# Order and sources of the first loads, casts and squares of a hybrid decoder trunk on one core

## Chip, core and metric

The kernel runs on one core of one Trainium2 chip. The metric is the device time of one execution in microseconds (us), the median of several runs; less is better. A profile of one execution, with every instruction's start and length and every DMA, is there as well.

## What is computed

The reference is a trunk of two layers over 528 positions (16 learned meta tokens ahead of 512 inputs) with 1024 features. Layer 0 is a sliding-window attention and a Mamba-2 scan side by side, layer 1 a convolution module; a squared-ReLU MLP follows each. What matters here is how layer 0 begins:

```python
h = jnp.concatenate([meta, x], axis=1)
u = rms_norm(h, norm_g)          # h * rsqrt(mean(h*h) + EPS) * norm_g
proj = u @ w_in                  # 1024 -> 3088 columns
q, k, v, z, xbc, dt_raw = jnp.split(proj, ...)
```

## The kernel before

All activations lie with features on the 128 partitions (8 feature tiles k) and positions along the free axis. Positions are cut into two streams: stream 0 has 272, stream 1 has 256 (STREAM, L28). Every large product is done in float32r with both operands cut into a high part and a low rest: hi·xh + hi·xl + lo·xh, that is 3 matmuls per feature tile (`products`, L518: first the pairs hi·xh and hi·xl for each k, then the lo·xh of the same piece). A weight comes in pieces of 4 feature tiles (256 KB): a DMA into a buffer `wr`, a cast on ScalarE (ACT) into the high part `wh` (`th_cast`, L464), and a subtraction on VectorE (DVE) or GpSimd (POOL) for the low rest `wl` (`th_low`, L480). There are four buffers of each kind at this point; `wh` and `wl` are given back when TensorE (PE) has used the piece for both streams.

The input goes through the same split. `th_enter` (L663) makes, for each k of a stream, xh = h·g on ACT (L671) and xl = h·g − xh on DVE (L672); g is `norm_g`, of which the first 8 columns of `vec` are loaded ahead of everything else (L1883). `th_norm` (L681) squares each k on ACT and adds the squares up on DVE (`sumsq`, L637); `row_norm` (L594) sums over the partitions on PE, takes square root (ACT) and reciprocal (DVE), and spreads the result to a tile `rb`. The row factor is thus not applied to the input but to the products: `ev_in` (L773) multiplies a finished output tile by `rb` when both streams' `rb` are there, and only then the PSUM bank of the product is free. PSUM has 8 banks: 3 called "mm" and 2 called "at", which take the products here, and 3 called "bg" for background work such as `row_norm` and `th_dt`. `pmm` (L346) takes an "mm" bank, or a "bg" bank when `wide[0]` allows it.

`main` (L1637) starts with `warm` (L1628), matmuls of a zeroed tile into a bank that nothing reads. It then computes output tiles 0 and 1 for stream 0 (L1658), the same two for stream 1 (L1665), and each further tile for both streams in turn (L1672). `extra` (L1645) says which input loads go ahead of which weight piece; `th_load` (L443) issues all loads on one queue, SyncE's (SP).

The order of instructions on each engine is not written out by hand. Generators ("threads") yield operations with an estimated length, and `Sched.step` (L178) simulates the engines and emits the operation that could start first; among those that could start at the same time it takes the one whose thread has the lowest priority number. The estimate for a load is 1500 ns of latency, then 5.2 ns per KB one after the other, then 700 ns (L129, L298). These estimates thus decide the order of all later instructions of the program, not only of the loads.

Of the kernel before, what the change touches and what calls it, by code (L numbers as in the profile page):

```python
# [9 lines left out]
F32 = mybir.dt.float32  # L10
F32R = mybir.dt.float32r
BF16 = mybir.dt.bfloat16
AF = mybir.ActivationFunctionType
# [226 lines left out]
def trunk(ctx: ExitStack, tc: tile.TileContext, h0, vecs, cmat, atab, atab0, w_in, w_dt, w_out,  # L240
# [20 lines left out]
    def TT(o, a, b, op, pool=False):  # L261
        n = cols(o)
        ways = [("V", 1.04 * n + 145, lambda: nc.vector.tensor_tensor(o, a, b, op=op), sb(a) and sb(b))]  # L263
        if pool:
            ways.append(("G", 2.17 * n + 170, lambda: nc.gpsimd.tensor_tensor(o, a, b, op=op), True))  # L265
        return Op(ways, [o], [a, b])
# [12 lines left out]
    def VEC(ns, fn, o, *inp, port=False):  # L279
        return Op([("V", ns, fn, port)], o if isinstance(o, list) else [o], list(inp))  # L280
# [7 lines left out]
    def CP(o, a):  # L288
        return Op([("A", 0.836 * cols(o) + 192, lambda: nc.scalar.copy(o, a), False)], [o], [a])  # L289
# [5 lines left out]
        return Op([("G", 1.1 * cols(o) + 170, lambda: nc.gpsimd.tensor_copy(o, a), True)], [o], [a])  # L295

    def DMA(o, a, kb):
        return Op([("S", kb * 5.2, lambda: nc.sync.dma_start(o, a), False)], aps(o) if sb(o) and o.tensor.name in S.mem else [],  # L298
                  [a] if a.tensor.name in S.mem else [])

    def load(o, a, kb):
# [39 lines left out]
    def bank(tag, name):  # L341
        return take(ps, [128, 512], F32, tag, BANKS[tag], name)
# [81 lines left out]
    def th_sum():  # L424
        i = 0
        while True:
            yield lambda: i < len(plan) or over
            if i >= len(plan):
                return
            if plan[i][3] == "sum":  # L430
                op, (a, x), (b, y) = plan[i][1]
                yield lambda: a in raws and b in raws
                t = yield take(wm, [128, 4, 128], F32, "raw", 4, "ws")
                o = TT(t, raws[a][:, x:x + 4], raws[b][:, y:y + 4], op, True)
                o.ways[0] += (bias[0] / 2,)
                yield o
                raws[i] = t
                used_raw(a, b)
            i += 1

    extra = {}

    def th_load():  # L443
        i = 0
        while True:
            yield lambda: i < len(plan) and plan[i][0] in POOLS or over
            if over and i >= len(plan):
                return
            for g in extra.pop(i, ()):
                yield from g  # L450
            pool, src, n, kind = plan[i]
            if kind in (None, "raw"):
                p, nraw, nsplit, w = POOLS[pool]
                raw = yield take(p, [128, w, 128], F32, "raw", nraw, "wr")
                yield DMA(raw[:, :n], src, 64 * n)
                raws[i] = raw
            i += 1

# [5 lines left out]
    def th_cast():  # L464
        i = 0
        while True:
            yield lambda: i < len(plan) or over
            if i >= len(plan):
                return
            if plan[i][3] != "raw":  # L470
                j, src = source(i)
                yield lambda: j in raws
                pool, _, n, _ = plan[i]
                p, nraw, nsplit, w = POOLS[pool]
                hi = yield take(p, [128, w, 128], F32R, "hi", nsplit, "wh")
                yield CP(hi[:, :n], src())
                his[i] = hi
            i += 1

    def th_low():  # L480
        i = 0
        while True:
            yield lambda: i < len(plan) or over
            if i >= len(plan):
                return
            if plan[i][3] != "raw":
                yield lambda: i in his
                pool, _, n, _ = plan[i]
                p, nraw, nsplit, w = POOLS[pool]
                lo = yield take(p, [128, w, 128], F32R, "lo", nsplit, "wl")  # L490
                j, src = source(i)
                hi = his.pop(i)
                o = TT(lo[:, :n], src(), hi[:, :n].bitcast(F32), ALU.subtract, True)
                o.ways[0] += (bias[0],)
                yield o
                used_raw(j)
                ready[i] = (hi, lo)
                split[0] += 1
            i += 1
# [122 lines left out]
    def par(gens, prio, name):  # L622

        left = [0]

        def run(g):
            yield from g
            left[0] -= 1
        for g in gens:
            left[0] += 1  # L630
            spawn(run(g), prio, name)
        yield lambda: left[0] == 0

    def after(*names):
        return lambda: all(n in done for n in names)
# [27 lines left out]
    def th_enter(s):  # L663

        n = STREAM[s][1]

        def one_(k):
            g = V("g_mix", k)
            hk = hin[s][:, k, :n]
            yield after(f"hin{s}{k}")  # L670
            yield ACT(xh[s][:, k, :n], hk, AF.Copy, scale=g)  # L671
            yield STT(xl[s][:, k, :n], hk, g, xh[s][:, k, :n].bitcast(F32), ALU.mult, ALU.subtract)  # L672
            entered[s].add(k)
        yield from par([one_(k) for k in range(8)], 2 * s, "enter")
        yield after(f"sq{s}")
        drop(hin[s])
        sz[s] = yield K(f"kl{s}", F32, f"sz{s}")
# [3 lines left out]
    def th_norm(s):  # L681
        n = STREAM[s][1]
        begun = []

        def one_(k):
            yield after(f"hin{s}{k}")
            yield from sumsq(acc[s], hin[s][:, k, :n], k == 0, begun)
        yield from par([one_(k) for k in range(8)], 1 + 2 * s, "norm")
        done.add(f"sq{s}")
        r = yield from row_norm(s, acc[s], BLOCKS[s], 1e-6, f"in{s}")  # L690
        done.add(f"rb{s}")
        yield VCP(rtok[:, BLOCKS[s][0]:BLOCKS[s][-1] + 1], r)
        done.add(f"rtok{s}")
# [558 lines left out]
    def load_h(s, k, n):  # L1252
        c0, w = STREAM[s]
        yield load(hin[s][:, k:k + n, :w], h0[:, k:k + n, c0:c0 + w], 0.5 * n * w)
        for j in range(k, k + n):
            done.add(f"hin{s}{j}")
# [371 lines left out]
    def warm():  # L1628

        z = at.rearrange("p h k -> p (h k)")[:, 0:512]  # L1630
        yield VEC(300, lambda: nc.vector.memset(z, 0.0), z)
        p = yield bank("at", "warm")
        for _ in range(11):
            yield Op([("P", 430, lambda: nc.tensor.matmul(p, lhsT=z[:, 0:128], rhs=z, start=True, stop=True), False)], [p], [z])
        drop(p)

    def main():  # L1637
# [4 lines left out]
        expect([w_out[n, :, 4:] for n in range(8)], 8)  # L1642
        plan_mlp(0, 0, 2, 4, 2, 4)
        plan_mlp(0, 1, 0, 0, 2, 4)
        extra.update({0: [load_h(0, 0, 1)], 1: [load_h(0, 1, 1), load_h(0, 2, 2)], 2: [load_h(0, 4, 2), load_h(0, 6, 2)],  # L1645
                      4: [load_h(1, 0, 2), load_h(1, 2, 2), load_h(1, 4, 2), load_h(1, 6, 2), load_const()],
                      5: [run_th(th_dtw(), "dtw")], 8: [run_th(tables(), "tables")]})
        for s in range(2):
# [6 lines left out]
        spawn(th_ssd_norm(), 1, "ssd_norm")  # L1655
        X = [(xh[s], xl[s], 0, STREAM[s][1]) for s in range(2)]
        lead = []
        for n in range(2):  # L1658
            p = yield bank("mm", "in")
            pcs = []  # L1660
            for k in (0, 4):
                pcs.append((yield from piece()))
                yield from products(p, pcs[-1], k, range(k, k + 4), 8, X[0], 0, lambda k: k in entered[0])
            lead.append((p, pcs))
        for n in range(2):  # L1665
            p, pcs = lead[n]
            q = yield bank("at", "in")
            for k, pc in zip((0, 4), pcs):
                yield from products(q, pc, k, range(k, k + 4), 8, X[1], 0, lambda k: k in entered[1])
                done_with(*pc[:2])  # L1670
            spawn(ev_in(n, (p, q)), 1, "inev")
        for n in ORDER[2:]:  # L1672
            b, pcs = [], []
            for s in range(2):
                p = yield bank("mm", "in")
                b.append(p)
                for i, k in enumerate((0, 4)):
                    if s == 0:
                        pcs.append((yield from piece()))
                    yield from products(p, pcs[i], k, range(k, k + 4), 8, X[s])  # L1680
                    if s:
                        done_with(*pcs[i][:2])
            spawn(ev_in(n, b), 1, "inev")
# [196 lines left out]
        yield from mlp(1, 3, [(*F[0], *AH[0], None), (*F[1], *AH[1], None)], last=fin_part)  # L1880

    with tc.manual_schedule():
        nc.sync.dma_start(vec[:, 0:8], vecs[:, 0:8])  # L1883
        S.part(vec)[0][0][:, :8] = 2500.0
        for g, p, n in ((main(), 5, "main"), (th_load(), 0, "load"), (th_cast(), 1, "cast"), (th_sum(), 1, "sum"),
                        (th_low(), lambda: 1 if split[0] - used[0] < 3 else 4, "low")):
            spawn(g, p, n)
        while S.threads:
            S.step()
# [84 lines left out]
```

## Time and profile before

| | |
|---|---|
| runs of the kernel before | 1229.56 us median of 3 (1229.52 to 1231.16) |
| profiled execution | 1230.29 us, of which the span from first to last instruction is 1228.5 us |
| PE busy | 1213.2 us (99% of the span) |
| DVE, ACT, POOL busy | 869.2, 714.7, 532.5 us |
| bytes moved by DMA | 185.98 MB, mean 151 GB/s |
| mean granted TensorE clock | 0.997 |

Times within the profile count from the first instruction. In a row of the timeline stand: start, length in us, engine, line, operation, output and inputs by the program's names, shapes, a count, and in square brackets the idle time ahead of it and what ended it. A row with a count covers that many instructions and its length is from the first's start to the last's end. Consecutive instructions of an engine overlap, so that the distance of two starts is shorter than one length. A row of the chain of waits has start, length and what was on the chain.

### The profile page before, as it was taken

How to read it: one execution, taken by the hardware profiler on the slowest of the kernel's cores; microseconds unless marked ns; L12 is line 12 of the kernel's file. 1: busy time of each engine (PE TensorE's matmuls, PEld its weight loads, DVE VectorE, ACT ScalarE, POOL GpSimd, SP SyncE). 2: the span in 40 equal slices, each digit the busy share in tenths (PEclk: the TensorE clock that was granted, in tenths of full speed). 3: DMA queues.
4: the chain of work that ended last, by engine and by line, in shares of the span. 5: the costliest groups of instructions: out<-in, count | busy, mean ns of one | idle time of the engine just before them, and what ended most of it. 6: DMA issues, size and time to landing. Idle time of an engine off the chain costs nothing.

```text
span 1228.5 us, 25576 instructions
## 1 busy us (share of the span) xinstructions
PE 1213.2 (99%) x9891; PEld 1169.4 (95%) x9891; DVE 869.2 (71%) x1921; ACT 714.7 (58%) x1391; POOL 532.5 (43%) x335
## 2 busy tenths in 40 slices
PE   8999999899999999999999999999999999999998
PEld 7999887689999999999999999999999999999998
DVE  6745686776876575748999735499996676666687
ACT  7654246767665654564664677557556665544452
POOL 0212331352542121158888788788887600000123
PEclk9999999999999999999999999999999999999999
DMA  6323112335445765546565565565555656556222
GB/s 192 106 81 89 41 37 77 97 96 163 130 146 182 235 194 165 185 125 194 184 189 175 170 190 176 178 200 175 180 181 174 192 159 194 189 183 190 87 62 94
DMA packets 76793, 185.98 MB, mean 151 GB/s; under 512 B 8560, under 2 KB 16256, under 8 KB 76672
## 3 DMA queue, kind: packets, MB, share of 16 engines
q1 hardware_dynamic: 76672, 184.36, 48.8%
q8 instruction: 77, 1.26, 0.4%
q14 instruction: 44, 0.36, 0.1%
HBM read 182.23 MB, written 2.10 MB: 150 GB/s over the span
## 4 chain that ended last, share of the span: by engine, by line
PE 93%; ACT 3%; DVE 3%; issue 1%; DMA 0%; SPq 0%; DVEq 0%; ACTq 0%
PE in L317 12%; PE pw L317 9%; PE out L317 6%; PE up13AB L317 4%; PE dn13AB L317 3%; PE dn00A L317 2%; PE up01A L317 2%; PE up02A L317 2%; PE dn01A L317 2%; PE up00A L317 2%; PE up03A L317 2%; PE dn02A L317 2%; PE dn02B L317 2%; PE up10A L317 2%; PE up12A L317 2%; PE dn12B L317 2%
## 5 line engine op out<-in xcount | busy, mean ns | idle before, releaser
L265 POOL TENSOR_TENSOR wl<-wr,wh 128x512 fp32r<-128x512 f32 x275 | 486.8, 1788 | 579.4 <-ACT wh L289 501.2
L289 ACT CAST wh<-wr 128x512 fp32r<-128x512 f32 (+1 forms) x472 | 367.6, 797 | 244.4 <-issue 27.5
L263 DVE TENSOR_TENSOR wl<-wr,wh 128x512 fp32r<-128x512 f32 (+1 forms) x197 | 183.8, 943 | 94.7 <-ACT wh L289 92.6
L270 DVE SCALAR_TENSOR_TENSOR conv<-U,vec,conv 128x256 f32<-128x256 f32 x464 | 209.2, 486 | 9.6 <-ACT conv L285 2.7
L317 PE MATMUL in<-xh,wh 128*128 128x272 f32 (+1 forms) x384 | 104.0, 297 | 1.5 <-ACT wh L289 1.5
L317 PE MATMUL in<-xl,wh 128*128 128x272 f32 (+1 forms) x384 | 100.9, 289 | 1.3 <-DVE xl L270 1.3
L317 PE MATMUL pw<-nh,wh 128*128 128x256 f32 (+1 forms) x320 | 80.7, 286 | 0.1
L317 PE MATMUL pw<-nl,wh 128*128 128x256 f32 (+1 forms) x320 | 80.2, 284 | 0.0
L317 PEld LDWEIGHTS in<-xh,wh 128*128 128x128 f32 x384 | 73.4, 191 | 6.8 <-issue 3.4
L317 PEld LDWEIGHTS in<-xl,wh 128*128 128x128 f32 x384 | 73.5, 191 | 2.5 <-DVE xl L270 2.1
L317 PE MATMUL in<-xh,wl 128*128 128x272 f32 (+1 forms) x384 | 66.5, 291 | 0.0
L317 PEld LDWEIGHTS pw<-nh,wh 128*128 128x128 f32 x320 | 60.2, 188 | 0.5 <-ACT sqh L285 0.3
L317 PEld LDWEIGHTS pw<-nl,wh 128*128 128x128 f32 x320 | 60.3, 189 | 0.0
L317 PEld LDWEIGHTS in<-xh,wl 128*128 128x128 f32 x384 | 54.8, 192 | 1.5 <-issue 0.7
L317 PE MATMUL pw<-nh,wl 128*128 128x256 f32 (+1 forms) x320 | 48.1, 284 | 0.0
L317 PEld LDWEIGHTS pw<-nh,wl 128*128 128x128 f32 x320 | 42.7, 188 | 0.0
L285 ACT ACT_TABLE_LOAD x30 | 38.5, 1283 | 5.5 <-DMA hin<-in_h 3.9
L317 PE MATMUL out<-xh,wh 128*128 128x272 f32 (+1 forms) x128 | 33.3, 289 | 0.5 <-ACT h L289 0.5
L317 PE MATMUL out<-xl,wh 128*128 128x272 f32 (+1 forms) x128 | 32.7, 284 | 0.0
L263 DVE TENSOR_TENSOR pw<-pw,rb 128x272 f32<-128x272 f32 (+1 forms) x32 | 14.0, 439 | 26.0 <-PE pw L317 25.7
L317 PE MATMUL up13AB<-nl,wh 128*128 128x256 f32 x128 | 31.1, 281 | 0.0
L317 PE MATMUL up13AB<-nh,wh 128*128 128x256 f32 x128 | 31.1, 281 | 0.0
(604 smaller groups left out, 3667.9 us busy)
## 6 DMA issues: line engine op xcount, KB each, us to landing
wr<-in_w_dn SPq DMA_DIRECT2D x80, 512.0 KB, 3.9
wr<-in_w_up SPq DMA_DIRECT2D x78, 512.0 KB, 3.6
wr<-in_w_up SPq DMA_DIRECT2D x84, 256.0 KB, 4.3
wr<-in_w_dn SPq DMA_DIRECT2D x80, 256.0 KB, 4.0
wr<-in_w_p SPq DMA_DIRECT2D x36, 512.0 KB, 3.7
wr<-in_w_in SPq DMA_DIRECT2D x48, 256.0 KB, 2.9
wr<-in_w_out SPq DMA_DIRECT2D x36, 256.0 KB, 2.7
wr<-in_w_p SPq DMA_DIRECT2D x24, 256.0 KB, 4.7
```

Source lines behind the costliest of these rows:

```text
L263: ways = [("V", 1.04 * n + 145, lambda: nc.vector.tensor_tensor(o, a, b, op=op), sb(a) and sb(b))]
L265: ways.append(("G", 2.17 * n + 170, lambda: nc.gpsimd.tensor_tensor(o, a, b, op=op), True))
L270: lambda: nc.vector.scalar_tensor_tensor(o, a, s, b, op0=op0, op1=op1), sb(a) and sb(b))],
L285: return Op([("A", ns, lambda: nc.scalar.activation(o, a, f, **kw), False)], aps(o, accum), aps(a, scale, bias), table=TABLE.get(f, 0))
L289: return Op([("A", 0.836 * cols(o) + 192, lambda: nc.scalar.copy(o, a), False)], [o], [a])
L317: nc.tensor.matmul(o, lhsT=l, rhs=r, start=st, stop=sp)
```

## The change

- `warm`: after the zero tile is set, ACT takes the square root of one column of it; 8 matmuls of zeros instead of 11.
- The first 8 columns of `vec` (the norm's scales, 4 KB) are loaded by ACT's queue instead of SP's.
- The first weight piece is loaded, cast and subtracted in two halves of two feature tiles; the load of k = 1 of stream 0 goes between the halves.
- `th_norm`: the squares of stream 0 may begin when all 8 tiles of stream 0 and 2 of stream 1 are split, those of stream 1 when all of both are. Before, a square could begin as soon as its tile had landed.
- Priorities: the split of stream 1 goes from 2 to 0.8, the casts from 1 to 0.7.
- The third output tile may take one "bg" bank for its second stream.
- The estimate of a load goes from 5.2 to 3.4 ns per KB, for every load of the program.
- `for n in range(2)` becomes `ORDER[:2]`, which holds the same two tiles.

```diff
     def DMA(o, a, kb):
-        return Op([("S", kb * 5.2, lambda: nc.sync.dma_start(o, a), False)], ...
+        return Op([("S", kb * 3.4, lambda: nc.sync.dma_start(o, a), False)], ...
...
+    def parts_of(i, n):
+
+        return ((0, n),) if i else ((0, n // 2), (n // 2, n))
...
-                yield DMA(raw[:, :n], src, 64 * n)
+                for a, b in parts_of(i, n):
+                    yield DMA(raw[:, a:b], src[:, a:b], 64 * (b - a))
+                    for g in extra.pop((i, b), ()):
+                        yield from g
...
-                yield CP(hi[:, :n], src())
+                for a, b in parts_of(i, n):
+                    yield CP(hi[:, a:b], src()[:, a:b])
...
-                o = TT(lo[:, :n], src(), hi[:, :n].bitcast(F32), ALU.subtract, True)
-                o.ways[0] += (bias[0],)
-                yield o
+                for a, b in parts_of(i, n):
+                    o = TT(lo[:, a:b], src()[:, a:b], hi[:, a:b].bitcast(F32), ALU.subtract, True)
+                    o.ways[0] += (bias[0],)
+                    yield o
...
-        yield from par([one_(k) for k in range(8)], 2 * s, "enter")
+        yield from par([one_(k) for k in range(8)], 0.8 * s, "enter")
...
         def one_(k):
-            yield after(f"hin{s}{k}")
+            yield lambda: len(entered[0]) == 8 and len(entered[1]) >= (8 if s else 2)
             yield from sumsq(acc[s], hin[s][:, k, :n], k == 0, begun)
...
         yield VEC(300, lambda: nc.vector.memset(z, 0.0), z)
+        yield ACT(small([128, 1], "then"), z[:, 0:1], AF.Sqrt)
         p = yield bank("at", "warm")
-        for _ in range(11):
+        for _ in range(8):
...
-        extra.update({0: [load_h(0, 0, 1)], 1: [load_h(0, 1, 1), load_h(0, 2, 2)], ...
+        extra.update({0: [load_h(0, 0, 1)], (0, 2): [load_h(0, 1, 1)], 1: [load_h(0, 2, 2)], ...
...
         for n in ORDER[2:]:
+            wide[0] = 1 if n == ORDER[2] else 0
             b, pcs = [], []
             for s in range(2):
-                p = yield bank("mm", "in")
+                p = yield pmm("in")
...
-        nc.sync.dma_start(vec[:, 0:8], vecs[:, 0:8])
+        nc.scalar.dma_start(vec[:, 0:8], vecs[:, 0:8])
...
-        for g, p, n in (... (th_cast(), 1, "cast"), ...
+        for g, p, n in (... (th_cast(), 0.7, "cast"), ...
```

More of the change, by code (lines that the diff above doesn't have):

```diff
@@ L297, in DMA @@
     def DMA(o, a, kb):
-        return Op([("S", kb * 5.2, lambda: nc.sync.dma_start(o, a), False)], aps(o) if sb(o) and o.tensor.name in S.mem else [],
+        return Op([("S", kb * 3.4, lambda: nc.sync.dma_start(o, a), False)], aps(o) if sb(o) and o.tensor.name in S.mem else [],
                   [a] if a.tensor.name in S.mem else [])
@@ L1644, in main @@
         plan_mlp(0, 1, 0, 0, 2, 4)
-        extra.update({0: [load_h(0, 0, 1)], 1: [load_h(0, 1, 1), load_h(0, 2, 2)], 2: [load_h(0, 4, 2), load_h(0, 6, 2)],
+        extra.update({0: [load_h(0, 0, 1)], (0, 2): [load_h(0, 1, 1)], 1: [load_h(0, 2, 2)], 2: [load_h(0, 4, 2), load_h(0, 6, 2)],
                       4: [load_h(1, 0, 2), load_h(1, 2, 2), load_h(1, 4, 2), load_h(1, 6, 2), load_const()],
@@ L1657, in main @@
         lead = []
-        for n in range(2):
+        for n in ORDER[:2]:
             p = yield bank("mm", "in")
@@ L1664, in main @@
             lead.append((p, pcs))
-        for n in range(2):
-            p, pcs = lead[n]
+        for n, (p, pcs) in zip(ORDER, lead):
             q = yield bank("at", "in")
@@ L1882, in trunk @@
     with tc.manual_schedule():
-        nc.sync.dma_start(vec[:, 0:8], vecs[:, 0:8])
+        nc.scalar.dma_start(vec[:, 0:8], vecs[:, 0:8])
         S.part(vec)[0][0][:, :8] = 2500.0
-        for g, p, n in ((main(), 5, "main"), (th_load(), 0, "load"), (th_cast(), 1, "cast"), (th_sum(), 1, "sum"),
+        for g, p, n in ((main(), 5, "main"), (th_load(), 0, "load"), (th_cast(), 0.7, "cast"), (th_sum(), 1, "sum"),
                         (th_low(), lambda: 1 if split[0] - used[0] < 3 else 4, "low")):
```

## The prediction

> **What bounds the kernel now.** I read the page first, for the share of each engine and the chain that ended last.
>
> ```profile
> PE 1213.2 (99%) x9891; PEld 1169.4 (95%) x9891; DVE 869.2 (71%) x1921; ACT 714.7 (58%) x1391; POOL 532.5 (43%) x335
> ...
> PE 93%; ACT 3%; DVE 3%; issue 1%; DMA 0%; SPq 0%; DVEq 0%; ACTq 0%
> ```
>
> PE is busy for 99% of the span and makes up 93% of the chain. No matmul of the computation goes away, so the change can only gain where PE stood idle, or ran at a lower clock. The busy times by stretch say where that is.
>
> ```profile
> 0.00:20.00 20.00, 16.02 (x85) 12.21 (x86) 13.87 (x34) 15.11 (x36) 0.20 (x4) 0.91 0.77 242
> 20.00:60.00 40.00, 39.93 (x331) 38.65 (x331) 30.70 (x77) 24.82 (x44) 7.83 (x12) 1.00 0.35 102
> ...
> 200.00:240.00 40.00, 36.42 (x252) 29.37 (x251) 27.06 (x95) 30.01 (x68) 11.42 (x9) 1.00 0.33 93
> ```
>
> The columns are the stretch, its length, then busy time of PE, of PE's weight loads, DVE, ACT, POOL, the granted clock, the DMA share and GB/s. PE misses 4.0 us in the first 20 us, though 3.9 us of what it does there is the zeros; 0.07 us in the next 40; and 3.58 us in one later stretch, from 200 to 240 us, which the change does not touch directly. So the entry is worth reading closely: PE's timeline there.
>
> ```profile
> 1.19 3.90 PE L1634 MATMUL warm<-at 128*128 128x512 bf16 x11 [1.19 <-DVE at L1631]
> 6.61 0.39 PE L317 MATMUL in<-xh,wh 128*128 128x272 f32 x1 [1.53 <-ACT wh L289]
> ...
> 11.24 0.43 PE L317 MATMUL in<-xh,wh 128*128 128x272 f32 x1
> 11.46 0.43 PE L317 MATMUL in<-xl,wh 128*128 128x272 f32 x1
> ...
> 14.35 0.29 PE L317 MATMUL in<-xl,wh 128*128 128x272 f32 x1
> 14.47 0.29 PE L317 MATMUL in<-xh,wh 128*128 128x272 f32 x1
> ...
> 16.98 0.28 PE L317 MATMUL in<-xh,wh 128*128 128x256 f32 x1
> 17.10 0.28 PE L317 MATMUL in<-xl,wh 128*128 128x256 f32 x1
> ```
>
> The first matmul of the computation starts at 6.61. At 16.98 the width goes from 272 to 256: stream 0 of tiles 0 and 1 is done, 2 tiles x 2 pieces x 12 = 48 matmuls. From start to start a 272-wide matmul takes 0.12 us at full speed (14.35 to 14.47; I use 0.125, so that 12 make 1.5 us) and a 256-wide one 0.12 (16.98 to 17.10). The 48 need 6.0 us and took 10.4. I therefore measure the change by one moment, T, at which stream 1 begins; before it is 16.98, and after it PE has work without a gap until about 26 us. What T gains, the end gains, as long as nothing else stops PE.
>
> Part of the loss is the clock: between 11.24 and 11.46 the same matmul takes 0.22 us, and the granted clock says the same.
>
> ```profile
> 3.96:10.79 6.83, 4.09 (x18) 2.23 (x16) 4.60 (x11) 6.82 (x16) 0.00 (x0) 1.00 0.98 315
> 10.79:14.20 3.41, 3.36 (x13) 3.14 (x14) 3.31 (x9) 3.17 (x9) 0.00 (x0) 0.50 1.09 358
> ```
>
> Half the clock for 3.41 us, after 6.83 us in which PE was busy for 4.09. In those 6.83 us ACT is busy for 6.82 and DMA for 0.98 of the time: the entry is held by both. ACT's, DVE's and the load queue's rows:
>
> ```profile
> 3.92 1.28 ACT L285 ACT_TABLE_LOAD   x1 [3.92 <-DMA hin<-in_h]
> 5.21 0.52 ACT L285 ACTIVATE xh<-hin,vec 128x272 fp32r<-128x272 f32 x1
> 5.64 0.41 ACT L285 ACTIVATE acc<-hin 128x272 f32<-128x272 f32 x1
> 5.96 0.60 ACT L289 CAST wh<-wr 128x512 fp32r<-128x512 f32 x1
> ...
> 7.21 0.92 ACT L285 ACTIVATE xh<-hin,vec 128x272 fp32r<-128x272 f32 x2
> ```
>
> ```profile
> 5.77 0.50 DVE L270 SCALAR_TENSOR_TENSOR xl<-hin,vec,xh 128x272 fp32r<-128x272 f32 x1 [4.64 <-ACT xh L285]
> ...
> 14.15 0.69 DVE L263 TENSOR_TENSOR wl<-wr,wh 128x512 fp32r<-128x512 f32 x1
> ```
>
> ```profile
> 0.74 0.38 SPq L1883 DMA_DIRECT2D vec<-in_vecs  x1
> 1.17 0.42 SPq L298 DMA_DIRECT2D hin<-in_h  x1
> 1.64 0.42 SPq L298 DMA_DIRECT2D wr<-in_w_in  x1
> ...
> 3.57 0.95 SPq L298 DMA_DIRECT2D hin<-in_h  x2
> 4.56 1.14 SPq L298 DMA_DIRECT2D wr<-in_w_in  x2
> 5.74 2.85 SPq L298 DMA_DIRECT2D hin<-in_h  x4
> ```
>
> The list of DMA issues gives the time from issue to landing: first a group of the whole program, then, asked for the moments of single issues, the first weight piece (issued 1.64), the last input load of stream 0 (4.04), the third and fourth piece (4.56 and 5.07), stream 1's four.
>
> ```profile
> wr<-in_w_dn SPq DMA_DIRECT2D x80, 512.0 KB, 3.9
> ...
> wr<-in_w_in SPq DMA_DIRECT2D x1, 256.0 KB, 3.4
> hin<-in_h SPq DMA_DIRECT2D x1, 272.0 KB, 5.6
> wr<-in_w_in SPq DMA_DIRECT2D x2, 256.0 KB, 5.9
> hin<-in_h SPq DMA_DIRECT2D x4, 256.0 KB, 6.0
> ```
>
> So landings are at 3.9 for k = 0 (ACT's wait ends at 3.92), 5.0 for the first piece, 9.6 for k = 6 and 7, 10.5 and 11.0 for the last two pieces, up to 14.2 for stream 1 (last issue near 8.2).
>
> **The change, part by part.**
>
> *The scales on ACT's queue.* SP's first issue falls away, so every load starts 0.43 us earlier (1.17 less 0.74). The second half of the first piece adds one issue of 0.42 behind k = 1, so later issues stand where they stood. But DMA is busy 0.98 of the time from 3.96 on, and bytes that start earlier end earlier: I take 0.43 for all landings to 14 us. Bounds: 0 (if issue times rule the later ones) and 0.43. On ACT the issue costs about SP's 0.38, in time in which it waited for its first input (3.92). If that cover were gone, and the scales landed after k = 0, each tenth would delay the first xh by a tenth.
>
> *Table first.* The load of 1.28 us ran from 3.92 to 5.20, on the path. Now it runs once the zeros are set, from 1.2 to 2.5, with the square root, 0.2, behind it: ACT is idle to 3.5. Whether squares and copies need another table shows later in the trace.
>
> ```profile
> 372.20 1.28 ACT L285 ACT_TABLE_LOAD   x1
> ...
> 532.13 0.40 ACT L285 ACTIVATE sqh<-dn03A 128x272 f32<-128x272 f32 x1
> 534.78 0.20 ACT L285 ACTIVATE rs_tcn<-rs_vcn 128x3 f32<-128x3 f32 x1 [1.74 <-DVE rs_vcn L277]
> ```
>
> Square roots, squares and copies run there between one load and the next at 535.0. So one load serves the entry and the root of the norm, and the second one goes:
>
> ```profile
> 21.05 1.28 ACT L285 ACT_TABLE_LOAD   x1
> ...
> 27.33 0.39 ACT L289 COPY rb<-stin 128x272 f32<-128x272 f32 x1 [2.94 <-PE stin L317]
> ```
>
> *Halves.* A cast of 256 columns is under 0.39 us (the copy of 272 just shown) against 0.60. By bytes (132 KB more than k = 0's), half of the first piece lands half way between 3.9 and 5.0, at 4.45, less 0.43: 4.0. First xh from 3.5 to 4.0, cast to 4.4, first matmul near 4.5 instead of 6.61. Two halves cost ACT 0.18 more and DVE as much, while k = 2 and 3 are still on their way: nothing.
>
> *Eight zeros.* Eleven end at 5.09 (1.19 and 3.90), eight near 4.0 (8/11 of 3.90); with eleven, the first matmul would wait some 0.6 us, but k = 6 and 7 set T anyway. Worth 0.
>
> *Squares behind.* Eight squares and seven sums leave the path ahead of T. In the 6.83 us, ACT then has eight xh at about 0.42 and four casts (0.39 twice, 0.5 thrice): 5.7 us between 3.5 and 11.3. DMA is what is late next.
>
> *T, then.* k = 6 and 7 land at 9.2; two xh take 0.92, to 10.1; xl 0.50, to 10.6. PE owes the last matmul of that pair, 4 with the low weights and 24 of tile 1: 29 x 0.125 = 3.6. T = 14.3. The fourth piece lands at 10.6, is cast by 11.3 and its low part is there at 12.0 (0.69); PE wants it at 13.8: covered by 1.8. Stream 1 lands by 13.8, its last xl is there at 15.2; PE wants it about 2.1 us after T, 16.4: covered by 1.2. The gain is 16.98 - 14.3 = 2.7 us; with landings as before, 2.3.
>
> *Behind T.* The norm's chain kept PE idle once, before its spreading matmuls:
>
> ```profile
> 25.90 0.29 PE L317 MATMUL in<-xl,wh 128*128 128x272 f32 x1
> 26.26 1.03 PE L317 MATMUL stin<-cm,rs_rin 16*128 16x16 f32 x6
> ```
>
> 0.36 less 0.12, 0.24 us. With the table load gone from 21.05 I count 0.2 as gained (bounds 0 and 0.24). The bank for the third tile lets PE run 24 matmuls (2.8 us) further before a bank must be free.
>
> *The estimate of 3.4.* It moves the order of everything that follows. With it a lone 512 KB is 1.5 + 1.7 + 0.7 = 3.9 us; the row of the 80 such loads has 3.9, and 5.2 gave 4.9. A truer estimate may remove waits or make others; PE's idle 3.58 us between 200 and 240 is the largest stretch that order can change. I bound it by 3.6 either way and take 0, as no row leans to one side.
>
> Sum: 2.7 + 0.2 = 2.9 us. The profiled execution took 1230.29, which makes 1227.4; it lies 0.73 above the median of the runs, 1229.56, which makes **1226.7**.
>
> **Rivals.**
>
> *Half clock again.* In the changed entry PE does about 20 matmuls from 3.96 to 10.79, zeros among them, where the row counts 18. If that was too little, the clock is halved again from 10.79: of 29 matmuls, 15 pass by 14.2 at 0.225, 14 follow at 0.125: T = 15.95, a gain of 1.0, with the 0.2 a time of 1228.4. For it speaks that PE's load hardly changes; against it that other stretches with gaps (200 to 240) ran at 1.00. [...]
>
> *Later waits vanish.* If the new order removes the 3.58 us as well, 1223.1.
>
> *Slower: the norm comes too late.* Squares that start when two tiles of stream 1 are split (landed at 11.3, split by 12.7) instead of at 5.64 also end later; I put the sums of stream 0 at 4 us later than before. If the chain from there to `rb` is as long as before, `rb` moves from 27.3 to 31.3 and frees the first bank near 31.7. PE, begun at 14.3, has 48 matmuls of tiles 0 and 1 (5.6), 48 of the third tile (5.8) and about 2 of the norm: work to 27.8. The price is 3.9 us, which turns 2.9 into a loss of 1.0, 1230.6, and with the half clock (1.7 more) 1232.3. It begins when `rb` is later than 27.4 and eats up the gain at 30.3. Against it: the chain was long for want of order, not of time (the table load at 21.05 stands in it), and `th_dt`'s matmuls can fill in.
>
> *It doesn't do what it says.* The landings stay, DMA holds PE, and what ACT saved becomes waiting for loads: T near 16.5, 1229.2.
>
> **How the numbers follow.** Chances: forecast 0.50 (its own range 1225.3 to 1228.2), half clock 0.20, later waits vanish 0.12, late norm 0.10, no effect 0.08. The range runs from 1223.4, nearly all of the third case, to 1230.4, which leaves out most of the fourth. A measurement can tell about 0.2%, 2.5 us, from no change, so the bounds are 1227.1 and 1232.0. Faster: two thirds of the first case, the third, and a little of the second, 0.48. Slower: half of the late norm, with some for orders that turn out worse later, 0.10. Within: 0.42.
>
> **What would show it.** Right: a table load near 1.2 and 29 in all instead of 30; the first `in` matmul between 4.4 and 5; the first 256-wide one near 14.3; k = 6 and 7 landing near 9.2; no idle PE between 14.3 and 40; PE's busy time from 60 on as before. Wrong: a granted clock of 0.50 behind 10 us (half clock); `in` waiting for ACT `rb` or DVE `pad` near 28 (late norm); first input landing still at 3.9 or ACT waiting for `vec`; idle PE between 200 and 240 changed by over 1 us, in which case the estimate of loads outweighs the entry.

## The result, and the profile after

The changed kernel takes 1233.16 us (median of 10 runs, 1231.52 to 1234.89); the kernel before, run beside it, 1231.18 (10 runs, 1229.52 to 1233.74). The ratio is 1.0019, with a 95% interval of 1.0010 to 1.0028: about 2 us slower, where 2.9 us faster was forecast. (The forecast of 1226.7 started from 1229.56, the median of 3 runs; 1.6 us of its distance from 1233.16 lies in that base.) The profiled execution took 1234.07 us, with a span of 1232.3.

The changed kernel's page, engines' busy times, chain and table loads:

```profile
PE 1214.1 (99%) x9888; PEld 1169.5 (95%) x9888; DVE 864.2 (70%) x1915; ACT 711.7 (58%) x1389; POOL 544.1 (44%) x344
...
PE 92%; DVE 3%; ACT 2%; DMA 1%; issue 1%; SPq 0%; ACTq 0%; DVEq 0%
...
L285 ACT ACT_TABLE_LOAD x28 | 35.9, 1283 | 4.9 <-DVE Y L270 3.3
```

The averages hardly move. So the entry first, in the changed kernel's timeline of ACT:

```profile
0.73 0.41 ACTq L1893 DMA_DIRECT2D vec<-in_vecs  x1
1.17 1.28 ACT L285 ACT_TABLE_LOAD   x1 [1.17 <-PEq L1972]
2.46 0.20 ACT L285 ACTIVATE then<-at 128x1 f32<-128x1 bf16 x1
3.16 0.52 ACT L285 ACTIVATE xh<-hin,vec 128x272 fp32r<-128x272 f32 x1 [0.49 <-DMA vec<-in_vecs]
3.94 0.41 ACT L289 CAST wh<-wr 128x256 fp32r<-128x256 f32 x1 [0.26 <-DMA wr<-in_w_in]
...
9.22 0.93 ACT L285 ACTIVATE xh<-hin,vec 128x272 fp32r<-128x272 f32 x2 [0.33 <-DMA hin<-in_h]
```

and of PE:

```profile
4.40 0.60 PE L317 MATMUL in<-xh,wh 128*128 128x272 f32 x1
4.80 0.43 PE L317 MATMUL in<-xl,wh 128*128 128x272 f32 x1
...
14.65 0.66 PE L317 MATMUL in<-xh,wl 128*128 128x272 f32 x4
15.15 0.28 PE L317 MATMUL in<-xh,wh 128*128 128x256 f32 x1
```

The table load has gone ahead of the first input, the first matmul starts 2.2 us earlier than in the kernel before, and stream 1 (the first 256-wide matmul) at 15.15 instead of 16.98. The entry did win 1.8 us.

Where it went is read from PE's busy time in three later stretches. The changed kernel's:

```profile
200.00:240.00 40.00, 35.91 (x247) 28.87 (x243) 28.03 (x95) 29.69 (x70) 12.48 (x10) 1.00 0.36 99
280.00:300.00 20.00, 19.01 (x149) 18.54 (x148) 13.08 (x33) 15.01 (x36) 1.20 (x1) 1.00 0.47 137
425.00:450.00 25.00, 23.72 (x192) 23.50 (x191) 16.80 (x32) 16.31 (x32) 4.37 (x3) 1.00 0.66 215
1183.00:1202.00 19.00, 16.53 (x125) 16.13 (x124) 15.93 (x33) 8.92 (x20) 4.21 (x3) 0.91 0.25 84
```

The kernel before, in the last three:

```profile
280.00:300.00 20.00, 20.00 (x159) 19.73 (x158) 14.46 (x32) 14.50 (x34) 5.13 (x4) 1.00 0.52 153
425.00:450.00 25.00, 25.00 (x204) 25.00 (x204) 18.97 (x35) 16.77 (x35) 5.43 (x3) 1.00 0.67 212
1183.00:1202.00 19.00, 18.41 (x152) 17.91 (x152) 16.44 (x34) 9.54 (x18) 6.29 (x5) 1.00 0.38 111
```

Where PE had no idle time at all before (20.00 of 20, 25.00 of 25), it now misses 0.99 and 1.28 us, and near the end 2.47 instead of 0.59; the last stretch runs at a granted clock of 0.91 as well. The stretch from 200 to 240, the one that the prediction watched, misses 4.09 instead of 3.58. The changed kernel's waits of PE between 200 and 460 us (us in total, times, longest) name the two new ones:

```profile
PE up02A L317 <- DVE acc L263: 1.3, 1, 1.3
PE up00A L317 <- ACT wh L289: 1.0, 1, 1.0
```

To follow the whole program I match each matmul with its twin (the same tile, the same count) in the kernel before and subtract the starts. "Lead" is how much earlier the changed kernel is; the moments are starts in the kernel before.

| lead, us | stream 1 starts (16.98) | 40.8 | 279.5 | 453.6 | 1181.4 | end (1228.5) |
|---|---|---|---|---|---|---|
| the change | 1.83 | 1.15 | 2.66 | -1.11 | -1.23 | -3.77 |

It wins 1.83; loses 0.68 by 41 us; gains 1.51 between 41 and 280, where the profiled execution of the kernel before had a half-clock stretch from 123.43 to 126.84 and this one has none; loses 3.77 between 280 and 454; and loses 2.54 from 1181 to the end. With the 0.12 lost between 454 and 1181 the sum is the 3.77 between the spans of the two profiled executions. The two named waits are 2.3 of the 3.77 us lost between 280 and 454; no single wait accounts for the rest. The two big losses lie far from everything that the change touches, except the estimate of a load.

### The profile page after: what moved, and what is told of

It reads as the page before. It is cut to its first block, busy times and chain, and to the rows that moved or that the text cites. A ratio compares the mean times of both kernels' runs of the same rounds, so it can differ in the third digit from the quotient of the medians.

```text
span 1232.3 us, 25595 instructions
## 1 busy us (share of the span) xinstructions
PE 1214.1 (99%) x9888; PEld 1169.5 (95%) x9888; DVE 864.2 (70%) x1915; ACT 711.7 (58%) x1389; POOL 544.1 (44%) x344
## 4 chain that ended last, share of the span: by engine, by line
PE 92%; DVE 3%; ACT 2%; DMA 1%; issue 1%; SPq 0%; ACTq 0%; DVEq 0%
PE in L317 12%; PE pw L317 10%; PE out L317 5%; PE up13AB L317 4%; PE dn13AB L317 3%; PE up01A L317 2%; PE up00A L317 2%; PE dn01A L317 2%; PE up03A L317 2%; PE dn02A L317 2%; PE dn02B L317 2%; PE up10A L317 2%; PE up12A L317 2%; PE dn00A L317 2%; PE dn11A L317 2%; PE dn12B L317 2%
## 5 line engine op out<-in xcount | busy, mean ns | idle before, releaser
L265 POOL TENSOR_TENSOR wl<-wr,wh 128x1024 fp32r<-128x1024 f32 (+2 forms) x282 | 495.3, 1774 | 552.6 <-ACT wh L289 459.7
L289 ACT CAST wh<-wr 128x512 fp32r<-128x512 f32 (+2 forms) x473 | 366.6, 795 | 254.4 <-PE in L317 28.8
L263 DVE TENSOR_TENSOR wl<-wr,wh 128x512 fp32r<-128x512 f32 (+2 forms) x191 | 184.3, 973 | 93.9 <-ACT wh L289 87.1
```

## The experiments

**Theory:** the entry wins about what it shows, and the new estimate (3.4 ns per KB instead of 5.2), which reorders instructions of the whole program, loses more. **Rival 1:** the earlier entry itself makes the later waits. **Rival 2:** the half-clock stretches, which lie elsewhere in each execution, make the difference. A third possibility is that something in the first 40 us (norm, squares, zeros) costs.

The experiments come in three groups of four, in the order in which they stand here. The kernel before, run beside each group, took 1231.22 us (21 runs), 1230.65 (32) and 1230.86 (35), so a difference between times of two groups is uncertain by some 0.6 us.

### The estimate by itself

The change without its new estimate:

```diff
-        return Op([("S", kb * 3.4, lambda: nc.sync.dma_start(o, a), False)], ...
+        return Op([("S", kb * 5.2, lambda: nc.sync.dma_start(o, a), False)], ...
```

> The whole change, but the estimate of a load stays at 5.2 ns per KB. Where the planned orders are set side by side, this kernel has the order of the kernel before from 100 to 600 us and from 1000 us on; the changed kernel differs there. Theory: the entry gains about 2 us (first 256-wide matmul at 15.15 instead of 16.98, 2.64 us ahead at 147 us) and the later orders that the new estimate brings lose about 4.6. Then this one is 1.8 to 2.8 us faster than before (ratio 0.998), with PE ahead by about 2 us from 20 us to the end. Rival 1: the earlier start itself makes the later waits (work that comes early collides elsewhere); then this one is like the changed kernel, +2 us. Rival 2: the half-clock stretches, which lie elsewhere in each execution, make the difference; then it is within 1.7 us of both, without sign.

Measured: 1229.29 us (11 runs), ratio to the kernel before 0.9984 [0.9976, 0.9993]. This is 1.9 us below the kernel before and 3.9 below the changed kernel.

The kernel before with the new estimate alone (the same line, the other way round):

> The kernel before with nothing changed but the estimate of a load, 3.4 instead of 5.2 ns per KB. Theory (the orders lose): 3.5 to 5.5 us slower than before (ratio 1.0035), with PE falling behind at about 282 to 294 us, near 430 to 441 us, and from 1183 us on, and none of the entry's gain. Rival 1 (the earlier start makes the waits): within 1 us of before. Rival 2 (half-clock stretches): within 1.7 us, no sign.

Measured: 1235.35 us (5 runs), ratio 1.0035 [1.0022, 1.0047]. The estimate alone costs 4 us without any of the other edits. Its PE waits 1.0 us for ACT's `wh` near 288 as in the changed kernel, although it comes there 0.96 us late and not early, so rival 1 falls. Nor is it the clock (rival 2): runs with a mean granted clock of 0.997 take 1235.0 us (mean of 4), those of the kernel before 1230.1 (mean of 7). Not all that its profiled execution loses lies in the two places: 1.67 us are lost when stream 1 starts, in an entry at half the clock from 8.55 to 15.37, then 2.76 between 280 and 454, and 1.05 from 1181 on, there behind other waits than in the changed kernel (1.5 in total for DVE's `sq`, 0.7 for its `wl`).

### The entry of one kernel, the later order of the other

The planner follows a recorded order from the attention's output product on (about 200 us):

```diff
+        S.replay = True
         yield from out_proj(0, pr, True)
...
     def step(self):
...
+        if self.replay:
+            for th in self.threads:
...
+                j, e = self.order.get((th[5], th[6], th[7] + 1 + _SHIFT.get(th[5], 0)), (1 << 30, None))
```

First the changed kernel's beginning, then the order of the kernel before:

> The changed kernel up to the output projection of layer 0, then every thread's operations in the order, and on the engines, that the kernel before has (a table of that order stands in the kernel). Theory: PE is 2.6 us ahead when the output projection begins and keeps that to the end: 2 to 3 us faster than before. Rival 1: the later waits come back although the order is the old one, +2 us. Rival 2: between -1.7 and 1.7 without sign.

Measured: 1230.86 us (11 runs, 1227.81 to 1233.8), ratio 0.9997 [0.9986, 1.0009]. Less than expected, and the interval holds no change. Its stream 1 starts at 16.68, for PE ran at half the clock until 14.05; its runs with a mean granted clock of 0.998 or more take 1227.8 to 1230.4, the seven with 0.996 take 1230.4 to 1233.8. By itself it settles nothing.

The other way round, the beginning of the kernel before and then the changed kernel's order:

> The opposite: the kernel before up to the output projection of layer 0, then the order and engines of the changed kernel. Theory: no gain at the entry and the losses of the new order: 3.5 to 5.5 us slower than before. Rival 1: within 1 us of before. Rival 2: within 1.7 us without sign.

Measured: 1234.7 us (5 runs), ratio 1.0039 [1.0026, 1.0053]. With the old entry the new order loses as much as the estimate alone.

### Zeros and squares

These are built on the change with the old estimate (1229.29). Its timeline of PE showed something unforeseen:

```profile
12.73 0.43 PE L317 MATMUL in<-xh,wh 128*128 128x272 f32 x1
12.95 0.43 PE L317 MATMUL in<-xl,wh 128*128 128x272 f32 x1
13.18 0.36 PE L317 MATMUL in<-xh,wh 128*128 128x272 f32 x1
13.38 0.28 PE L317 MATMUL in<-xl,wh 128*128 128x272 f32 x1
13.50 0.29 PE L317 MATMUL in<-xh,wh 128*128 128x272 f32 x1
```

From start to start it is 0.22 us until 13.2 and 0.12 after: with eight zeros PE ran at half the clock until then in this execution. Stream 1 began at 16.01.

```diff
-        for _ in range(8):
+        for _ in range(11):
```

> The change with the old estimate of loads (5.2), and eleven zeros again instead of eight; the order of all other work is the same as with eight. Theory now (zeros are not worth 0): with eight zeros, which end near 4.8, the kernel with the old estimate ran at half the clock until 13.32, and stream 1 began at 16.0 instead of the 14.3 that I forecast; profiles with eleven zeros show the full clock from 4.0 to 5.1. So with eleven the clock is full before 5.5, may be halved once more between 8 and 14, and stream 1 begins between 14.4 and 15.4: 0.6 to 1.6 us earlier than with eight, the time 1228 to 1229 instead of 1229.3. Rival (zeros are worth 0, as predicted): stream 1 begins near 16 or at a moment that has nothing to do with the zeros, and the time stays within 0.3 us of 1229.3.

Measured: 1229.06 us (11 runs), ratio 0.9995 [0.9985, 1.0006]. Full clock from 3.87, stream 1 at 14.61.

The same with `range(16)`. At half the clock the zeros start 0.43 us apart (from 1.59 to 4.15 in the changed kernel), so sixteen would last some 6.9 us. The half-clock stretches of the kernel before last 3.41 us each, and its clock changes at moments (10.79, 14.20, 123.43, 126.84) that are whole multiples of 3.41 us apart; 3.41 us from one such moment on are called a window:

> The same with sixteen zeros, which last two windows of 3.4 us at half the clock. Theory: full clock by 5.5 whatever the moment at which the windows begin, the zeros end near 6.3, the first matmul of the computation waits for them (1.9 us later than with eight), but k = 6 and 7, landing at 9.2, set the start of stream 1: 14.3 to 15.0 if the zeros keep the clock from being halved again near 8 to 14, else near 15.5; the time 1227.6 to 1228.6 (1 to 1.7 below eight zeros). Rival (zeros are worth 0): the same time as with eight within 0.3 us. Second rival (the zeros hold the computation up): stream 1 begins 1 us or more later than with eleven, and the time is above that of eleven by as much.

Measured: 1228.44 us (11 runs), ratio 0.9987 [0.9975, 0.9999]. Full clock from 4.93, first matmul only at 6.29, yet stream 1 at 14.80. So the wait for the zeros cost stream 1 at most 0.2 us against eleven, and the clock is full in the rest of the entry. In time, however, eight, eleven and sixteen zeros have overlapping intervals: the gain of 1.2 to 1.4 us in the profiled entries is not established in the medians.

```diff
-            yield lambda: len(entered[0]) == 8 and len(entered[1]) >= (8 if s else 2)
+            yield after(f"hin{s}{k}")
```

> The change with the old estimate of loads and eight zeros, but each square of the input follows its own split as before. Theory (the norm comes late by the squares): the second copy rb of the norm comes 1.5 to 2.5 us earlier than the 32.9 of the change, PE's waits between 24 and 40 us, about 1.0 us with the old estimate, shrink to 0.3 or less, and what the start of stream 1 loses by the squares is less than 0.6, since the table load has left that stretch: 0.3 to 0.9 us faster than with the squares behind, 1228.4 to 1229.0. Rival (squares on the path, the reason why the change moved them): eight squares of 0.41 and seven sums push the last splits back by 1.5 us or more, stream 1 begins that much later, and the time is 1230 or more.

Measured: 1229.72 us (11 runs), ratio 0.9990 [0.9981, 0.9998]. Neither theory: nothing lost between stream 1 and 41 us (leads 0.38 and 0.57), but stream 1 began at 16.61, in an entry whose clock was halved from 8.34 to 15.17.

> Both edits at once: old estimate, sixteen zeros, squares as before. If both theories hold their gains add up: stream 1 from 14.5 to 15.3, no more than 0.3 us of waits to 40 us, 1227.0 to 1228.0, which is 3.2 to 4.2 below the kernel before. If the zeros are worth 0 and the squares too, 1229.3. If only one holds, that one's time.

Measured: 1228.71 us (11 runs), ratio 0.9986 [0.9977, 0.9995]. Stream 1 at 15.43, 0.63 later than with the squares behind; lead at 41 us 1.31, against 1.21 with the squares behind. Moving the squares gains 0.6 at stream 1 and gives all of it back by 41 us.

### Which part of the order

The planner's estimate depends on its own time, on top of the old estimate and sixteen zeros:

```diff
-        return Op([("S", kb * 5.2, ...
+        return Op([("S", kb * (3.4 if S.now < 200e3 else 5.2), ...
```

> The change with sixteen zeros and the old estimate of loads, 5.2, but the planner counts 3.4 for what it issues in its first 200 us; by the planned order of the instructions only the first 100 us differ from 5.2 throughout. Theory (the order of 200 to 450 us and of the last 30 us costs what the entry gains, the entry's own order costs nothing): within 0.5 us of the 1228.44 of sixteen zeros with 5.2. Rival (the estimate spoils the norm's order near 28 us, where the changed kernel loses 0.7 us): 0.5 to 1.0 us above it, and the loss shows between the start of stream 1 and 41 us.

Measured: 1228.79 us (12 runs), ratio 0.9986 [0.9977, 0.9996], 0.35 above sixteen zeros. Its profiled execution loses 0.54 us between stream 1 and 41 us, where sixteen zeros with 5.2 lose 0.98. The order of the first 100 us is not the cause.

The same with `3.4 if 200e3 < S.now < 600e3 else 5.2`:

> The same, with 3.4 only for what the planner issues between its 200th and 600th us; by the planned order only 200 to 450 us differ. In the profiles the changed kernel goes from 2.66 us ahead of the kernel before at 280 us to 1.11 behind at 454; with 5.2 and sixteen zeros it goes from 2.74 to 2.23 ahead. Theory: this stretch alone costs 3.3 us, the time is 1231.2 to 1232.2, and PE waits for ACT's wh near 288 (1.0) and for DVE's acc near 435 (1.3) as in the changed kernel. Rival (the waits come from orders earlier in the program, or from a state that only the whole new order brings about): within 0.5 us of 1228.44.

Measured: 1231.5 us (11 runs), ratio 1.0009 [1.0001, 1.0018], 3.06 above sixteen zeros (at a mean granted clock of 1.000 it is 1231.1, the mean of 5 runs, against 1228.4, the mean of 9). The wait near 288 is back. ACT's timeline there, with sixteen zeros and the old estimate:

```profile
285.27 0.60 ACT L289 CAST wh<-wr 128x512 fp32r<-128x512 f32 x1
285.78 0.38 ACT L285 ACTIVATE up00A<-up00A 128x272 f32<-128x272 f32 x1
286.09 0.60 ACT L289 CAST wh<-wr 128x512 fp32r<-128x512 f32 x1
286.60 0.37 ACT L289 CAST xh<-up00A 128x272 fp32r<-128x272 f32 x1
286.87 0.62 ACT L289 CAST wh<-wr 128x512 fp32r<-128x512 f32 x1
...
289.37 0.39 ACT L289 COPY rb<-stnx 128x272 f32<-128x272 f32 x1 [0.67 <-PE stnx L317]
```

ACT's timeline with 3.4 from 200 to 600:

```profile
288.01 0.39 ACT L289 COPY rb<-stnx 128x272 f32<-128x272 f32 x1 [0.86 <-PE stnx L317]
288.30 2.18 ACT L289 CAST wh<-wr 128x512 fp32r<-128x512 f32 x4
```

and PE's:

```profile
288.97 0.39 PE L317 MATMUL up00A<-nh,wh 128*128 128x272 f32 x1 [0.99 <-ACT wh L289]
```

Read the order, not the lengths. Before, three casts stand ahead of the norm's copy `rb`; now `rb` stands first, ACT waits 0.86 us for PE's `stnx`, and the casts queue behind it until PE has nothing left and waits 0.99 us. No load is late here: the last two pieces that are cast were issued at 284.38 and 284.95 and landed some 2.6 us later, before the casts begin at 288.30. The casts simply stand behind a waiting instruction.

The second wait, for DVE's `acc` near 434, did not come back as expected: it is 0.5 us here and 0.3 with sixteen zeros and 5.2, against 1.3 in the changed kernel, where DVE had just waited 1.14 us for a load (`ut`). So this wait belongs to the order by 0.2 us only; why the load came late there is not shown.

The same with `5.2 if S.now < 600e3 else 3.4`:

> The same, with 3.4 only from the planner's 600th us on; by the planned order only 1100 us to the end differs. The changed kernel loses 2.5 us net from 1181 us to the end, with a half-clock stretch of 3.4 us in it; with 5.2 and sixteen zeros 0.8 are lost there. Theory: this stretch costs 1.8 us with the half-clock stretch, 1230.2, and 0.2 to 0.8 without it, 1228.7 to 1229.2; PE waits for POOL's U and DVE's h in the tiles of dn13AB. Rival: the waits there came from the lateness of everything before, and the time is within 0.2 us of 1228.44.

Measured: 1231.72 us (11 runs), ratio 1.0010 [1.0001, 1.0018], 3.28 above sixteen zeros: the waits as expected, the size nearly twice the 1.8 (which the profiled execution does show: from 1181 us to the end it loses 2.56, sixteen zeros 0.76). But 3.28 is not the price of that order. In the profiled executions 1.16 of the difference has arisen by 280 us, where both kernels still have the same order: this one ran at half the clock from 235.50 to 238.92, the one with sixteen zeros did not. Runs lose more clock here: 8 of 11 have a mean granted clock of 0.997, against 9 of 11 at 1.000 with sixteen zeros, and the two at 0.999 take 1230.3. POOL's timeline with 3.4 from 600 on:

```profile
1188.92 1.82 POOL L265 TENSOR_TENSOR wl<-ws,wh 128x512 fp32r<-128x512 f32 x1 [8.78 <-ACT wh L289]
1190.71 1.00 POOL L265 TENSOR_TENSOR U<-sq,U 128x256 fp32r<-128x256 f32 x1
```

PE's:

```profile
1191.76 0.38 PE L317 MATMUL dn13AB<-U,wh 128*128 128x256 f32 x1 [0.61 <-POOL U L265]
...
1194.47 0.45 PE L317 MATMUL dn13AB<-ah,wh 128*128 128x256 f32 x1 [1.85 <-DVE h L263]
```

DVE's with sixteen zeros and the old estimate:

```profile
1184.67 0.75 DVE L263 TENSOR_TENSOR U<-sq,U 128x256 fp32r<-128x256 f32 x2
```

With the old order DVE makes both products `U` at 1184.67. With the new one POOL makes one of them, behind a `wl` of 1.82 us, done at 1191.7: PE waits 0.61 for it, and DVE's sums `h` come 1.85 us after PE wants them.

At last the change as it is, with sixteen zeros:

> The change as it is, 3.4 throughout, with sixteen zeros instead of eight. Theory (parts add up, and the zeros keep the clock up in the entry): 1228.44 and the parts above, 1231.9 to 1233.2, no half-clock stretch before 14 us, stream 1 begins near 14.5 instead of 15.15, and the time is 0.3 to 1.0 us below the 1233.16 of the change. Rival (zeros are worth 0): 1233.2 within 0.3.

Measured: 1233.64 us (12 runs), ratio 1.0027 [1.0017, 1.0037]. Stream 1 at 14.47, full clock throughout the entry, and still as slow as the change. The zeros don't mend what the order loses; the gain of 0.3 to 1.0 that I expected is not there. The parts (0.35, 3.06, 3.28) sum to 6.7 where the whole is 5.2 above sixteen zeros. They hold the clock as well as the order: a half-clock stretch near 1196 us, which the profile with 3.4 from 600 on has and this one has not, is 1.7 us of such a difference (3.41 at half).

| lead, us | stream 1 starts | 40.8 | 279.5 | 453.6 | 1181.4 | end |
|---|---|---|---|---|---|---|
| kernel before, 3.4 alone | -1.67 | -0.96 | -0.96 | -3.72 | -3.99 | -5.04 |
| 5.2, sixteen zeros | 2.19 | 1.21 | 2.74 | 2.23 | 2.09 | 1.33 |
| 3.4 from 200 to 600 | 2.34 | 1.37 | 2.11 | -0.88 | -1.01 | -1.19 |
| 3.4 from 600 on | 2.03 | 1.05 | 1.58 | 1.06 | 0.94 | -1.62 |
| 3.4, sixteen zeros | 2.51 | 1.96 | 2.64 | -0.95 | -1.08 | -2.13 |

Between 280 and 454 us only the kernels with 3.4 in that stretch lose (2.8, 3.0 and 3.6, the others 0.5), whatever their lead was when they came there. From 1181 us on, 3.4 costs 2.6 where a half-clock stretch follows the waits (from 600 on: 1194.65 to 1198.06, and the change likewise), and 1.05 where none does (the first and the last row), against 0.8 and 0.2 with 5.2 there. So the order itself is dear only in the first of the two places. In the second it costs some 0.3 to 0.9 us, and the larger part is the clock, which some executions have and others don't.

## Why the prediction was wrong

*The failed step is "The estimate of 3.4", where I wrote "I bound it by 3.6 either way and take 0, as no row leans to one side".* The bound was PE's idle time between 200 and 240 us, "the largest stretch that order can change". That is a bound on what a new order can win, not on what it can lose: an order can put a wait where PE had none. In the runs the estimate costs 1235.35 less 1231.2, 4.1 us, on the kernel before, and 1233.64 less 1228.44, 5.2 us, on the changed one (4.9 by the two ratios, 1.0027 and 0.9987). The order's part of it lies above all between 280 and 454 us, where PE had stood at 100%; near the end the order adds little and the clock more. Of the 2.5 us that the new order costs in the first stretch (3.0 less 0.5), 1.0 is the wait near 288; which waits make up the rest is not shown. And a load of 512 KB that the planner counts as 3.9 us, as the trace has it, did not make the order of the casts or of POOL's share better. Why the greedy planner orders them worse with the truer number the runs don't show.

*Scales, table, halves: right in time.* I gave the last pair of stream 0 landed at 9.2, its splits done at 10.1 (ACT) and 10.6 (DVE), the first matmul near 4.5. ACT's wait ends at 9.22, its two splits end at 10.15 (9.22 and 0.93), and the first matmul is at 4.40. Two table loads went (28 instead of 30), not one. One sign that I had named as wrong did come, ACT waiting for `vec`: the scales landed near 3.1 (0.73 and 2.4 us), 0.2 behind k = 0 (0.74 and 2.2), and the first split began at 3.16, still ahead of the 3.5 that I had.

*T: the rival "half clock again" came.* Forecast 14.3, or 15.95 with the half clock; it was 15.15. The changed kernel's windows, in the entry and near the end:

```profile
5.36:8.77 3.41, 2.32 (x10) 1.58 (x11) 2.19 (x5) 2.91 (x7) 0.75 (x1) 1.00 1.02 340
8.77:12.18 3.41, 3.41 (x15) 2.91 (x14) 3.14 (x7) 2.98 (x8) 0.00 (x0) 0.50 1.07 367
...
1193.20:1196.61 3.41, 0.97 (x7) 0.65 (x5) 3.41 (x7) 0.62 (x1) 2.10 (x2) 1.00 0.51 179
1196.61:1200.02 3.41, 3.39 (x16) 3.39 (x17) 3.41 (x7) 0.37 (x1) 0.00 (x0) 0.50 0.47 157
```

Half a clock from 8.77 instead of 10.79, so that, as I read it, part of it fell on time in which the loads set the pace (the last split is done at 10.70): 0.85 us over the forecast instead of 1.65. Where the clock stayed full from 6.9 us at the latest (six profiles with eleven or sixteen zeros and the squares behind) T was 14.47 to 14.96, 0.2 to 0.7 over the forecast: the sum of the entry holds about that well.

*"Eight zeros ... Worth 0": not safe.* I priced them by whether the first matmul waits, and not by the clock behind them, which in two of the four profiles with eight zeros was half until 13.32 and 14.05. Their length was off for the same reason: 8/11 of 3.90 takes all eleven as equally long, but in the kernel before they start 0.43 us apart up to 3.72 and 0.21 apart from 4.06 on (the full clock is recorded from 3.96), so the last ones are shorter; the eight took 3.59 and ended at 4.78, not near 4.0. In single executions they moved T by over 1 us; in the medians no difference is established.

*"Behind T": wrong sign.* Instead of 0.2 won, 0.68 were lost by 41 us. PE now misses 0.48 us between stream 1 and 40 us, against 0.07 before. Its waits between 14 and 41 us in the changed kernel:

```profile
PE in L317 <- ACT dtr L289: 0.3, 1, 0.3
PE dt_a L317 <- ACT dtr L289: 0.2, 1, 0.2
```

and in the change with the old estimate and sixteen zeros:

```profile
PE in L317 <- DVE pad L263: 0.9, 1, 0.9
```

The rows of `rb` on ACT in the changed kernel:

```profile
28.26 0.39 ACT L289 COPY rb<-stin 128x272 f32<-128x272 f32 x1 [1.15 <-PE stin L317]
...
32.91 0.37 ACT L289 COPY rb<-stin 128x256 f32<-128x256 f32 x1
```

In the kernel before the two copies stand at 27.33 and 30.63. The rival "the norm comes too late" followed the first copy, to 31.3, though a bank is free only when both copies are there; the first came 0.9 us later and the second 2.3. In the changed kernel PE did not wait for `rb` or `pad`, the sign that I had named, but for the copies `dtr` of `th_dt`, and the loss was 0.7, not 3.9. The named sign, a wait for `pad`, is there with sixteen zeros and the old estimate, at 0.9 us. Squares put back took the loss after T away and gave it back before T.

*Rival "later waits vanish":* the missing PE time from 200 to 240 us went from 3.58 to 4.09, so it did not. I had also named a change there of over 1 us as the sign that the estimate outweighs the entry; it changed by 0.5, and the estimate outweighed the entry all the same, in stretches that I did not watch. *Slower* had a chance of 0.10, for a norm that comes late "with some for orders that turn out worse later"; the second was nearly the whole of it.

## What to carry to other kernels

When a kernel's order comes from a planner, an edit of the planner's numbers is a change of the whole program: test it apart from the edit that it comes with, and bound its cost by where PE is fully busy, not by where it is idle. A truer estimate need not give a better order. In the new trace look for what stands in front of the late instruction on its engine (`rb` ahead of the casts, `wl` ahead of `U`), before looking for a late load; but look for that too, as `ut` near 433 us shows.

## What the runs showed of the hardware

Behind the first recorded change of the clock, half-clock stretches last 3.41 us or twice that, and come at places that shift from profile to profile: in the entry (at 8.34, 8.55, 8.77 or 10.79), between 121 and 125, near 236, and at 1194.65 or 1196.61. In the changed kernel too the recorded changes (8.77, 12.18, 1196.61, 1200.02) are whole multiples of 3.41 us apart. What halves the clock is not shown. The stretch at 1196.61, which costs half its length, 1.7 us, stands behind a window with PE busy for 0.97 of 3.41 us; but in the kernel before the clock was halved at 123.43 with PE counted as busy all the time in the window ahead, though 12 of the matmuls in it have only 2 or 64 columns. The half-clock stretch stands first, then the window ahead of it:

```profile
123.43:126.84 3.41, 3.41 (x17) 3.07 (x17) 0.60 (x4) 1.42 (x2) 0.53 (x2) 0.50 0.00 1
120.02:123.43 3.41, 3.41 (x26) 2.50 (x23) 1.26 (x5) 2.10 (x3) 1.77 (x3) 1.00 0.52 156
```

PE's busy time in the window ahead does not decide it alone. Near 236 us seven of the fourteen profiles have a half-clock stretch, each behind a window with PE busy for 1.71 to 1.73 us; in four others, the kernel before among them (1.73 from 236.06 to 239.48), a window with the same busy time has none behind it. Two windows that begin at the same moment, with sixteen zeros and 5.2:

```profile
233.62:237.03 3.41, 1.73 (x13) 1.73 (x14) 2.96 (x12) 3.41 (x13) 0.59 (x1) 1.00 0.61 164
237.03:240.45 3.42, 2.91 (x22) 2.40 (x22) 3.02 (x6) 1.78 (x8) 1.04 (x1) 1.00 0.74 220
```

and with eight zeros, 5.2 and the squares as before:

```profile
233.62:237.04 3.42, 1.73 (x14) 1.38 (x14) 2.65 (x13) 3.42 (x12) 1.28 (x2) 1.00 0.52 150
237.04:240.45 3.41, 3.41 (x18) 3.41 (x17) 2.27 (x5) 2.47 (x10) 0.36 (x1) 0.50 0.66 171
```

With eight zeros, 3.6 us of them, the clock stayed at half until 13.32 and 14.05 in two of the four profiled kernels (in the other two it was full from 5.36 and 4.93); with sixteen it became full between 4.92 and 7.16 in all six, in five of them later than the 5.5 that I had expected. One execution of each can't say how often. The mean granted clock of a run tells part of the spread: beside the kernel with sixteen zeros the kernel before took 1229.2 us at 1.000 (mean of 6 runs) and 1231.7 at 0.996 (13 runs). The column of the granted clock says 1.00 ahead of the first recorded change, also where steps of 0.22 us show half of it; there the steps count.
